# Relative bias rows stored three heads at a time, in blocks two to four of stage one

## The chip, the cores and the metric

One core of a Trainium2 chip runs the whole program in one launch. The metric is the device time of that core in microseconds. Three runs of the kernel before gave 3175.7, 3193.27 and 3194.81 us, median 3193.27. The engines are PE (TensorE, matmuls; PEld is its weight load), DVE (VectorE), ACT (ScalarE), POOL (GpSimd) and SP (SyncE), which issues nearly all DMAs here, in one queue and in program order.

## The reference

One layer of a hybrid encoder over 2048 prompt tokens and 8 x 16 sample tokens, width 1024, everything in float32. What the change touches is the bias of group B's attention: a learned value per head and clipped relative distance.

```python
def rel_bias_matrix(rel_bias, qpos, kpos):
    d = jnp.clip(qpos[:, None] - kpos[None, :], -(CHUNK - 1), REL_MAX) + (CHUNK - 1)
    return rel_bias.astype(jnp.float32)[:, d]
...
s = jnp.einsum('bqhd,bkhd->bhqk', qc, kc).astype(jnp.float32) * (DH ** -0.5) + bias
```

There are 8 heads, and `rel_bias` has 320 values a head. Around it the layer is: modulation of the norm by a conditioning vector, one projection `h @ w_in` (1024 x 3592), a gated delta rule with a causal convolution on group A, band attention on group B, `w_out`, and a feed-forward of width 4096 with squared ReLU.

## The kernel before, in words

Float32 matmuls are made of three products each: every operand is split into a high and a low part, and `mm3` (L162 to L164) or its written-out copies (L519 to L521, L1482 to L1484) multiply high by high, high by low and low by high.

**Weights** come in pieces of 512 KB (`weights`, from L165). SP loads the float32 piece into a ring of three tiles `raw` (L174), ACT casts the high part into a ring of four tiles `w` (L175), and POOL subtracts to get the low part (L82). In the first block SP also stores the low parts of `w_in` in DRAM (L184, `s_w_in`); later blocks load these back (L179) and POOL does not subtract again.

**Stage one** (`phase1`) opens with the modulation vectors out of `w_mod` (pieces `raw0`, loaded at L282), then goes through 17 token tiles of 128 in six blocks: [0, 1, sample], [2, 3, 4], [5, 6, 7], [8, 9, 10], [11, 12, 13], [14, 15]; `bi` is the index of the block. For a block, `proj_a` makes group A's projections: first the gates of one half (`psg`, whose results go to DRAM as `s_sg` at L500), then 12 column pieces (`psq`, 24 matmuls of 128x384 each), each followed on DVE and ACT by the convolution (L79, tile `y`) and on PE by transposes (`ptq`, L554). `proj_b` makes group B's. Blocks three and five hold back their `proj_b`. The gated delta rule of a block (`gdn`) runs as a background lane among the next block's matmuls. The token tiles of the next block are loaded (L373, tile `x`), normed (statistics `bst` on DVE at L378, the root on POOL, the scaling on ACT), transposed (L346, `psh`) into tiles `htmp`, a ring of two, and split into the one tile `hT`, which all matmuls of the block read. PSUM has a ring of three tiles for the results of matmuls.

**Stage two** (`phase2`) does attention, `w_out` and the feed-forward for five blocks of tiles. It reads the bias rows: `bias<-s_bias` from 896.8 us on, `bias_s<-s_bs` at 2464.0 us.

**The bias table.** `rel_bias` (from L1092, called at L1062 once, at block two) loads all eight heads' rows (L1097), lays them out reversed and extended to 768 values a head in a tile of the ring `big` (a memset at L1098, copies on DVE at L1099 and L1100), writes this to DRAM (`s_ext`, L1101), and from there two DMAs from DRAM to DRAM spread it: `s_bias` (L1102, for each head 128 rows of 640 values, each row starting one value earlier) and `s_bs` (L1103, for each head 16 rows of 528).

**Order.** The kernel is written as one program; a scheduler then sets the order on every engine by its own estimate of times, and starts work early where its tile's ring is free. The ring `big` is not used before the first solve, so the scheduler moved the table of block two to the very start of the program, among the modulation's loads.

Of the kernel before, what the change touches and what calls it, by code (L numbers as in the profile page):

```python
# [8 lines left out]
F32 = mybir.dt.float32  # L9
# [5 lines left out]
P = 128  # L15
D = 1024
# [5 lines left out]
SL = 16  # L22
AH = 4
BH = 8
# [4 lines left out]
REL = 320  # L29
EXT = 768  # L30
# [11 lines left out]
def bcast(ap, axis, n):  # L42
    dims = [list(x) for x in ap.ap]
    dims.insert(axis, [0, n])
    return bass.AP(tensor=ap.tensor, offset=ap.offset, ap=dims)


def dram_ap(ap, offset, dims):
    return bass.AP(tensor=ap.tensor, offset=ap.offset + offset, ap=[list(d) for d in dims])


class Trunk:
# [975 lines left out]
    def phase1(self):  # L1028
        nc, tc = self.nc, self.tc
        with ExitStack() as st:  # L1030
            P_ = lambda name, **kw: st.enter_context(tc.tile_pool(name=name, bufs=1, **kw))
            right = ExitStack()
            R_ = lambda name, bufs=1, **kw: right.enter_context(tc.tile_pool(name=name, bufs=bufs, side="right", **kw))
            self.p1, self.hp, self.qp = (P_(x) for x in ("p1c", "p1h", "p1q"))
            self.bp = R_("p1b")
            self.ps = R_("p1ps", 3, space=bass.MemoryType.PSUM)
            pst = ExitStack()
            self.pa = pst.enter_context(tc.tile_pool(name="p1pa", bufs=5 - GP, side="right", space=bass.MemoryType.PSUM))
            self.patag = "pa"
            self.nt = max(len(b) for b in BLOCKS1)  # L1040
            self.nx, self.nA, self.inplace = 3, 4, True
            self.hT = self.p1.tile([P, KT, 2, self.nt * P], F32R, name="hT1")
            with tc.tile_pool(name="p0", bufs=1, side="right") as p0:
                xs = self.modulation_start([(sec, q, u) for q in range(4) for sec in (1, 0) for u in range(2)],
                                           BLOCKS1[0], p0)
            self.mod_todo = [(sec, q, u) for sec in (2, 3, 4, 5) for q in range(4) for u in range(2)]
            self.tp = R_("p1t")
            self.cp = pst.enter_context(tc.tile_pool(name="p1a", bufs=1, side="right"))
            self.phase1_consts()
            S0 = self.tp.tile([P, AH, P], F32, tag="S", name="S", bufs=1)  # L1050
            nc.vector.memset(S0, 0.0)
            self.S = S0
            B = BLOCKS1
            ca = lambda b: 24 * (512 + 1536) * len(B[b])
            cb = lambda b: 24 * 1536 * len(B[b])
            last = len(B) - 1
            self.load_hT(B[0], xs, 0, 1)
            for bi, tiles in enumerate(B):
                self.bi = bi
                self.keep["w_in"] = bi == 0  # L1060
                if bi == 1:
                    self.rel_bias()  # L1062
                self.drain_to(bi - 2)
                self.mix = bi == last
                blk = self.proj_a(tiles, self.hT, B[bi + 1] if bi in LATE else ())
                if bi == last:
                    break
                self.gdn(blk, tiles, bi)
                self.pace(0.95 * (cb(bi) * (bi not in LATE) + ca(bi + 1)), 6000)
                if bi not in LATE:  # L1070
                    self.proj_b(tiles, self.hT, B[bi + 1])
            pst.close()
            self.pa = R_("p1pa2", 1, space=bass.MemoryType.PSUM)
            self.ap2 = R_("p1att", 1, space=bass.MemoryType.PSUM)
            self.ap = R_("p1at")
            self.queue(self.attention_first(BLOCKS2[0]), 1 + BH + BH // 2 * len(BLOCKS2[0]) + BH + 2, lane=2)
            self.queue(self.conv_gen(), 6, lane=1)
            self.gdn(blk, tiles, last)
            rest = [last] + list(LATE)
            self.pace(0.85 * sum(cb(b) for b in rest))  # L1080
            for b, nb in zip(rest, rest[1:] + [None]):
                self.mix = b == last
                self.proj_b(B[b], self.hT, B[nb] if nb is not None else ())
            self.drain()
            nc.sync.dma_start(self.o["gdn_prompt"][0, 0].rearrange("h k v -> k h v"), self.S)
            right.close()
        self.pa, self.patag = self.gp, "g"
        self.ap = self.ctx.enter_context(tc.tile_pool(name="p2a", bufs=1, side="right"))
        self.ap2 = self.ctx.enter_context(tc.tile_pool(name="p2att", bufs=1, space=bass.MemoryType.PSUM, side="right"))


    def rel_bias(self):  # L1092

        nc = self.nc
        x = self.hp.tile([P, D], F32, tag="big", name="ext", bufs=2)
        ext, rev = x[0:BH, 0:REL], x[32:32 + BH, 0:EXT]
        nc.sync.dma_start(ext, self.i["rel_bias"][0])  # L1097
        nc.vector.memset(rev[:, EXT - 64:], 0.0)  # L1098
        nc.vector.tensor_copy(rev[:, EXT - 64 - REL:EXT - 64], ext[:, ::-1])  # L1099
        nc.vector.tensor_copy(rev[:, 0:EXT - 64 - REL], bcast(ext[:, REL - 1], 1, EXT - 64 - REL))  # L1100
        nc.sync.dma_start(self.s_ext, rev)  # L1101
        nc.sync.dma_start(self.s_bias, dram_ap(self.s_ext, P, [[EXT, BH], [-1, P], [1, 640]]))  # L1102
        nc.sync.dma_start(self.s_bs, dram_ap(self.s_ext, P, [[EXT, BH], [-1, SL], [1, 528]]))  # L1103

    def softmax(self, ap, ps, bias, n):

# [494 lines left out]
```

## Time and profile before

| | us |
|---|---|
| median of three runs | 3193.27 (3175.7 to 3194.81) |
| the profiled execution, its own time | 3181.62 |
| its span, first to last instruction | 3179.9 |
| PE busy in the span | 3046.9 (96%) |
| DVE / ACT / POOL busy | 1764.0 / 1472.8 / 644.5 |

The profile is one execution taken by the hardware profiler. Busy time of an engine excludes waits. A wait is put down to what released it. "DMA share" is the mean busy share of the 16 DMA engines, and PEclk the granted TensorE clock as a part of full speed. The mean granted clock of this execution is 0.985.

### The profile page before, as it was taken

The page shows a single profiled execution, that of the slowest core. Times are in us where ns is not written, and L with a number is a line of the kernel's source. Part 1 is how long each engine was busy: PE and PEld are TensorE (multiplying, and loading weights), DVE is VectorE, ACT ScalarE, POOL GpSimd, SP SyncE. Part 2 cuts the span into 40 slices and gives each one's busy share as a digit, 9 for nine tenths or more (in the row PEclk, how much of TensorE's full clock was granted, in tenths as well). Part 3 has the DMA queues.
Part 4 walks back from the last instruction along what each step waited for, and adds up shares of the span by engine and source line. Part 5 has one row for each costly group of instructions (what it writes and reads, how often), then busy time and mean ns, then how long its engine had stood idle before and what let it go on. Part 6 is the DMA issues. An engine that isn't in the chain of part 4 may idle for free.

```text
span 3179.9 us, 52984 instructions
## 1 busy us (share of the span) xinstructions
PE 3046.9 (96%) x19649; PEld 2701.7 (85%) x19649; DVE 1764.0 (55%) x4222; ACT 1472.8 (46%) x2803; POOL 644.5 (20%) x517
## 2 busy tenths in 40 slices
PE   6999999999889989999999999999999999999998
PEld 4998989899889878888999888888988877888887
DVE  4775677667878663674356752454745433442223
ACT  3654545555466555545455353444354333333222
POOL 3631211121342247653222200000000000000000
PEclk9999999999999989999999999999999999999999
DMA  8798897888788778876777765666666676856654
GB/s 289 239 294 268 258 284 228 253 250 248 234 268 264 214 229 277 254 250 231 253 238 244 238 214 181 197 193 204 232 198 200 214 236 219 273 173 194 193 190 139
DMA packets 625947, 735.88 MB, mean 231 GB/s; under 512 B 59328, under 2 KB 483248, under 8 KB 623640
## 3 DMA queue, kind: packets, MB, share of 16 engines
q1 hardware_dynamic: 619928, 701.03, 70.1%
q0 software_dynamic: 5760, 31.46, 3.0%
q8 instruction: 155, 2.54, 0.3%
q14 instruction: 104, 0.85, 0.1%
HBM read 619.74 MB, written 115.52 MB: 231 GB/s over the span
## 4 chain that ended last, share of the span: by engine, by line
PE 70%; DMA 13%; DVE 9%; issue 3%; ACT 3%; POOL 1%; SPq 1%; POOLq 0%; ACTq 0%; DVEq 0%
PE psu L1483 7%; PE psu L1482 7%; PE psu L1484 7%; PE psd L164 7%; PE psd L162 7%; PE psd L163 7%; PE psb L163 2%; DMA raw<-in_w_up_dram 2%; PE psb L162 2%; PE psb L164 2%; PE pv L1286 2%; PE psS L1268 2%; PE psq L519 1%; PE psq L521 1%; PE psq L520 1%
## 5 line engine op out<-in xcount | busy, mean ns | idle before, releaser
L175 ACT CAST w<-raw 128x1024 fp32r<-128x1024 f32 (+1 forms) x528 | 552.1, 1047 | 387.1 <-PE psd L164 214.1
L1482 PE MATMUL psu<-hT,w 128*128 128x512 f32 (+2 forms) x1328 | 470.1, 356 | 1.9 <-ACT hT L104 1.7
L1484 PE MATMUL psu<-hT,w 128*128 128x512 f32 (+2 forms) x1328 | 468.5, 354 | 1.4 <-DMA w<-s_w_up 1.4
L1483 PE MATMUL psu<-hT,w 128*128 128x512 f32 (+2 forms) x1328 | 469.2, 354 | 0.4 <-DVE hT L82 0.3
L82 POOL TENSOR_TENSOR w<-raw,w 128x1024 fp32r<-128x1024 f32 (+1 forms) x162 | 391.6, 2427 | 351.3 <-ACT w L175 285.3
L162 PE MATMUL psd<-w,u 128*128 128x512 f32 x1088 | 430.9, 396 | 0.4 <-DVE y L82 0.3
L164 PE MATMUL psd<-w,u 128*128 128x512 f32 x1088 | 429.8, 396 | 0.0
L163 PE MATMUL psd<-w,u 128*128 128x512 f32 x1088 | 426.8, 392 | 2.1 <-POOL w L82 2.1
L79 DVE SCALAR_TENSOR_TENSOR psu<-psu,r 128x512 f32<-128x512 f32 (+2 forms) x160 | 98.9, 618 | 447.0 <-ACT r L92 446.9
L82 DVE TENSOR_TENSOR y<-y,psd 128x512 f32<-128x512 f32 x238 | 162.4, 685 | 260.3 <-PE psd L164 259.3
L1484 PEld LDWEIGHTS psu<-hT,w 128*128 128x128 f32 x1328 | 250.5, 189 | 33.2 <-DMA w<-s_w_up 1.7
L1482 PEld LDWEIGHTS psu<-hT,w 128*128 128x128 f32 x1328 | 250.1, 189 | 33.0 <-ACT hT L104 2.5
L1483 PEld LDWEIGHTS psu<-hT,w 128*128 128x128 f32 x1328 | 250.7, 189 | 31.9 <-issue 1.3
L92 ACT ACTIVATE r<-psu 128x512 f32<-128x512 f32 (+2 forms) x160 | 85.4, 534 | 375.7 <-issue 214.0
L163 PEld LDWEIGHTS psd<-w,u 128*128 128x128 f32 x1088 | 204.6, 188 | 47.8 <-POOL w L82 2.8
L164 PEld LDWEIGHTS psd<-w,u 128*128 128x128 f32 x1088 | 204.2, 188 | 46.4 <-issue 0.4
L162 PEld LDWEIGHTS psd<-w,u 128*128 128x128 f32 x1088 | 204.4, 188 | 43.8 <-DVE y L82 1.0
L162 PE MATMUL psb<-w,hT 128*128 128x256 f32 x816 | 236.0, 290 | 0.9 <-ACT hT L104 0.8
L163 PE MATMUL psb<-w,hT 128*128 128x256 f32 x816 | 234.7, 288 | 0.9 <-DMA w<-s_w_in 0.9
L164 PE MATMUL psb<-w,hT 128*128 128x256 f32 x816 | 233.4, 286 | 1.9 <-DVE hT L82 1.8
L519 PE MATMUL psq<-hT,w 128*128 128x384 f32 (+1 forms) x576 | 196.9, 342 | 8.1 <-ACT ba L499 8.1
L521 PE MATMUL psq<-hT,w 128*128 128x384 f32 (+1 forms) x576 | 193.6, 336 | 0.2 <-DMA w<-s_w_in 0.2
(315 smaller groups left out, 6459.5 us busy)
## 6 DMA issues: line engine op xcount, KB each, us to landing
raw<-in_w_up_dram SPq DMA_DIRECT2D x160, 512.0 KB
raw<-in_w_down_dram SPq DMA_DIRECT2D x160, 512.0 KB
raw<-in_w_in_dram SPq DMA_DIRECT2D x156, 512.0 KB
w<-s_w_down SPq DMA_DIRECT2D x128, 512.0 KB
w<-s_w_in SPq DMA_DIRECT2D x117, 512.0 KB
w<-s_w_up SPq DMA_DIRECT2D x96, 512.0 KB
raw<-in_w_out_dram SPq DMA_DIRECT2D x40, 512.0 KB
x<-in_x_prompt_dram SPq DMA_DIRECT2D x38, 512.0 KB
```

The costliest lines, as they stand in the source:

```text
L79: (eng or self.nc.vector).scalar_tensor_tensor(out, in0, scalar, in1, op0, op1)
L82: (eng or self.nc.vector).tensor_tensor(out, in0, in1, op)
L92: self.nc.scalar.activation(out, in_, func, **kw)
L162: mm(out, lh, rh, start=first, stop=False)
L163: mm(out, lh, rl, start=False, stop=False)
L164: mm(out, ll, rh, start=False, stop=last)
L175: nc.scalar.copy(w[:, 0, 0:n], r)
L519: mm(pc, wh, hT[:, k, 0, 0:T], start=(k == 0), stop=False)
L521: mm(pc, wl, hT[:, k, 0, 0:T], start=False, stop=(k == KT - 1))
L1482: mm(ps[:, c0:c1], wh, h2[:, k, 0, c0:c1], start=(k == 0), stop=False)
L1483: mm(ps[:, c0:c1], wh, h2[:, k, 1, c0:c1], start=False, stop=False)
L1484: mm(ps[:, c0:c1], wl, h2[:, k, 0, c0:c1], start=False, stop=(k == KT - 1))
```

## The change

The table is made in three calls, at the starts of blocks two, three and four, for heads 0 to 2, 3 to 5 and 6 to 7. The tile is now one of the ring `htmp` (512 values a partition in place of 1024), so a head's 768 values lie in two partitions: 512 in `lo` and 256 in `hi`. Each call has one load, three copies and a memset on DVE, two writes to `s_ext`, and one DMA each into `s_bias` and `s_bs`. Bytes written to `s_bias` and `s_bs` are the same in sum.

```diff
-                if bi == 1:
-                    self.rel_bias()
+                if 1 <= bi <= 3:
+                    self.rel_bias(3 * bi - 3, min(3 * bi, BH))
...
-    def rel_bias(self):
+    def rel_bias(self, h0, h1):
...
-        x = self.hp.tile([P, D], F32, tag="big", name="ext", bufs=2)
-        ext, rev = x[0:BH, 0:REL], x[32:32 + BH, 0:EXT]
-        nc.sync.dma_start(ext, self.i["rel_bias"][0])
-        nc.vector.memset(rev[:, EXT - 64:], 0.0)
-        nc.vector.tensor_copy(rev[:, EXT - 64 - REL:EXT - 64], ext[:, ::-1])
-        nc.vector.tensor_copy(rev[:, 0:EXT - 64 - REL], bcast(ext[:, REL - 1], 1, EXT - 64 - REL))
-        nc.sync.dma_start(self.s_ext, rev)
-        nc.sync.dma_start(self.s_bias, dram_ap(self.s_ext, P, [[EXT, BH], [-1, P], [1, 640]]))
-        nc.sync.dma_start(self.s_bs, dram_ap(self.s_ext, P, [[EXT, BH], [-1, SL], [1, 528]]))
+        m, k = h1 - h0, EXT - 64 - REL
+        x = self.hp.tile([P, 4, P], F32, tag="htmp", name="ext", bufs=2).rearrange("p a b -> p (a b)")
+        ext, lo, hi = x[0:m, 0:REL], x[32:32 + m], x[64:64 + m, 0:EXT - 512]
+        rev = ext[:, ::-1]
+        nc.sync.dma_start(ext, self.i["rel_bias"][0][h0:h1])
+        nc.vector.tensor_copy(lo[:, 0:k], bcast(ext[:, REL - 1], 1, k))
+        nc.vector.tensor_copy(lo[:, k:], rev[:, 0:512 - k])
+        nc.vector.tensor_copy(hi[:, 0:EXT - 576], rev[:, 512 - k:])
+        nc.vector.memset(hi[:, EXT - 576:], 0.0)
+        nc.sync.dma_start(self.s_ext[h0:h1, 0:512], lo)
+        nc.sync.dma_start(self.s_ext[h0:h1, 512:], hi)
+        o = h0 * EXT + P
+        nc.sync.dma_start(self.s_bias[h0:h1], dram_ap(self.s_ext, o, [[EXT, m], [-1, P], [1, 640]]))
+        nc.sync.dma_start(self.s_bs[h0:h1], dram_ap(self.s_ext, o, [[EXT, m], [-1, SL], [1, 528]]))
```

In the changed kernel the lines of `rel_bias` are L1099 (load), L1100 to L1102 (copies), L1103 (memset), L1104 and L1105 (`s_ext`), L1107 (`s_bias`) and L1108 (`s_bs`).

What the scheduler made of it. On SP's queue near the start of the program, between the last loads for the modulation and the first weights, the difference is (minus: before only):

```order
 L174 DMA raw<-in_w_in_dram 128x4x264 x2
 L174 DMA raw<-in_w_in_dram 128x8x128
-L1097 DMA ext<-in_rel_bias_dram 8x320
 L282 DMA raw_207<-in_w_mod_dram 128x4x256
 L373 DMA x<-in_x_prompt_dram 128x1024
 L184 DMA s_w_in<-w 128x1056
 L174 DMA raw<-in_w_in_dram 128x8x128
-L1101 DMA s_ext<-ext 8x768
 L184 DMA s_w_in<-w 128x1056
 L174 DMA raw<-in_w_in_dram 128x8x128
```

The load of the rows and the write of the table are gone from here; some rows later so are the two DMAs that spread it (L1102 and L1103), which stood ahead of the third load of `x`.

On SP's queue of the changed kernel, in block two, at the first call (heads 0 to 2; `A<-s_U` are the solved 32x32 blocks of block one coming back, `s_sg` a gate of block two):

```order
L1104 DMA s_ext<-ext 3x512
L1105 DMA s_ext<-ext 3x256
L500 DMA s_sg<-sgw 128x256
L174 DMA raw<-in_w_in_dram 128x8x128
L179 DMA w<-s_w_in 128x1024
L174 DMA raw<-in_w_in_dram 128x8x128
L179 DMA w<-s_w_in 128x1024
L174 DMA raw<-in_w_in_dram 128x8x128
L1107 DMA s_bias<-s_ext 384x1x640
L1108 DMA s_bs<-s_ext 48x1x528
L666 DMA A<-s_U 32x4x32 x12
L560 DMA s_kt<-kvw 128x128 x3
```

In the kernel before, the same place has the gate, the weights and `A<-s_U` and nothing else. The second and third calls stand in the same way at the gates (`s_sg`) of blocks three and four.

On DVE of the changed kernel, at the same call (`ta` and `Ds` are the solve of block one, `sgw` the last gate of block two, `y` the first convolution of block two):

```order
L82 TENSOR_TENSOR ta<-Z,Ds 128x16
L82 TENSOR_TENSOR Ds<-Ds,ta 128x16
L79 SCALAR_TENSOR_TENSOR sgw<-th,psg 128x256
L1100 COPY ext<-ext 3x384
L1101 COPY ext<-ext 3x128
L1102 COPY ext<-ext 3x192
L79 SCALAR_TENSOR_TENSOR y<-psq,cw,y 128x384
```

Before, the convolution followed the gate at once. The rest of the order differs in many places from the second column piece of block one until the second block of stage two, since the scheduler set it anew; the kinds and numbers of matmuls are the same.

## Rows read from the trace of the kernel before

**Rows 1.** The page's part 1, busy time by engine.
```profile
PE 3046.9 (96%) x19649; PEld 2701.7 (85%) x19649; DVE 1764.0 (55%) x4222; ACT 1472.8 (46%) x2803; POOL 644.5 (20%) x517
```

**Rows 2.** Chain of waits, 28 to 100 us: start, us, what.
```profile
33.54 7.19 DMA ext<-in_rel_bias_dram
...
40.76 2.60 DVE ext L1099
43.36 2.41 DVE ext L1100
...
46.84 1.11 PE psh L346 x4
...
62.39 13.29 DMA x<-in_x_prompt_dram
...
78.10 0.34 DVE sgw L79
```

**Rows 3.** Timeline of all engines, 36 to 48 us.
```profile
38.38 7.19 POOL L82 TENSOR_TENSOR w<-raw,w 128x1056 fp32r<-128x1056 f32 x3 [8.95 <-ACT w L175]
...
42.08 1.08 PE L288 MATMUL mps<-raw,cT 128*32 128x256 f32 x8 [2.90 <-DMA raw<-in_w_mod_dram]
```

**Rows 4.** Timeline of SP's queue, 0 to 90 us: start, time to issue.
```profile
33.54 2.21 SPq L1097 DMA_DIRECT2D ext<-in_rel_bias_dram  x1
...
50.38 0.84 SPq L1102 DMA_DIRECT2D s_bias<-s_ext  x1
51.28 8.49 SPq L1103 DMA_DIRECT2D s_bs<-s_ext  x1
...
62.39 5.70 SPq L373 DMA_DIRECT2D x<-in_x_prompt_dram  x1
```

**Rows 5.** DMA issues by line, 0 to 100 us.
```profile
s_bias<-s_ext SPq DMA_DIRECT2D x1, 2560.0 KB
...
s_bs<-s_ext SPq DMA_DIRECT2D x1, 264.0 KB
```

**Rows 6.** Timeline of PE, 64 to 100 us.
```profile
70.25 0.33 PE L521 MATMUL psq<-hT,w 128*128 128x384 f32 x1
78.68 0.69 PE L519 MATMUL psq<-hT,w 128*128 128x384 f32 x1 [8.10 <-ACT ba L499]
...
82.61 0.34 PE L519 MATMUL psq<-hT,w 128*128 128x384 f32 x1
...
84.54 0.34 PE L521 MATMUL psq<-hT,w 128*128 128x384 f32 x1
```

**Rows 7.** Stretches: busy us by engine, granted clock, DMA share, GB/s.
```profile
57.00:62.00 5.00, 3.53 (x21) 3.06 (x22) 3.50 (x10) 2.92 (x7) 0.56 (x1) 1.00 0.52 207
...
70.00:79.00 9.00, 0.90 (x5) 0.58 (x4) 3.29 (x7) 2.63 (x9) 2.35 (x1) 0.81 1.00 342
...
100.00:150.00 50.00, 50.00 (x342) 49.36 (x341) 36.11 (x87) 30.53 (x89) 31.30 (x15) 1.00 0.73 227
...
215.00:235.00 20.00, 20.00 (x125) 19.34 (x124) 13.80 (x50) 10.66 (x26) 2.04 (x2) 1.00 1.09 324
...
385.00:410.00 25.00, 25.00 (x155) 22.98 (x154) 16.79 (x54) 8.17 (x18) 3.86 (x3) 1.00 1.01 303
...
485.00:515.00 30.00, 29.95 (x271) 28.74 (x270) 21.01 (x63) 17.54 (x44) 2.06 (x2) 1.00 0.75 219
```

**Rows 8.** Chain of waits, 0 to 250 us: loads of weights in block two.
```profile
207.62 6.85 DMA w<-s_w_in
...
230.02 5.98 DMA raw<-in_w_in_dram
...
242.74 8.42 DMA raw<-in_w_in_dram
```

**Rows 9.** What PE waited for, whole span: us, times, longest.
```profile
PE psb L163 <- DMA w<-s_w_in: 0.9, 1, 0.9
...
PE psq L521 <- DMA w<-s_w_in: 0.2, 1, 0.2
```

## The prediction

> **What bounds the kernel now.** I read the page's busy times first, then the chain of waits at the start (where the table is made), then the timelines of PE, DVE and SP around it, then the stretches into which the three new calls fall. PE is busy 3046.9 of 3179.9 us [rows 1], so only the 133.0 us in which it stands can be won, and anything new that stops it is paid in full. From 100 to 150 us PE is busy all the time [rows 7]; the start is not like that. There the chain of waits runs through the bias table itself: it waits for the load of the rows (7.19 us), stands through the two copies on DVE (2.60 and 2.41 us), and later waits 13.29 us for a load of `x` that was issued behind the table's spreading [rows 2]. PE stands for 8.10 us at 78.68 [rows 6]. In the stretches of the new calls PE loses nothing: 20.00 of 20, 25.00 of 25 and 29.95 of 30 us, but the DMA engines are full in two of them, 1.09 and 1.01, and 0.75 in the third [rows 7].
>
> **What goes from the start.** Three terms.
>
> First, the copies. DVE is in order, and behind the two copies stands the norm's scaling of `htmp`, on which PE's transposes at 46.84 wait [rows 2]. Without the copies PE is ready for these when its previous matmuls end, 42.08 + 1.08 = 43.16 [rows 3]. That is 46.84 - 43.16 = 3.7 us. POOL's subtractions in the same stretch [rows 3] go on as before and aren't waited for there.
>
> Second, the load of `x`. SP spends 0.84 us on the issue of `s_bias` and 8.49 us on that of `s_bs`, and the load of `x` is issued only at 62.39 [rows 4], behind 2560 + 264 KB of the table [rows 5]. DVE stands at its statistics until it lands at 62.39 + 13.29 = 75.68; the third gate behind it is done at 78.44, and only that frees a PSUM tile for PE at 78.68 [rows 2, 6]. Without the table the load is issued some 9 us earlier and has 2.8 MB less ahead of it; at 342 GB/s [rows 7] these alone are 8.5 us. So the 8.10 us go. Something new is late next: in the new order the small gate arithmetic of block one, which PE now needs after its third column piece, stands on DVE behind the same statistics, ahead of the results that free PSUM. I take 2 us for that, so this term is 6.1; its bounds are 0 (the gate arithmetic takes it all) and 8.1.
>
> Third, the slow matmuls after the stop. From 78.68 to 82.61 PE makes 12 matmuls in 3.93 us, and from 82.61 to 84.54 eleven in 1.93, or 0.175 each [rows 6]. The granted clock of 70 to 79 us is 0.81 [rows 7], a mean of the two levels (2.4 and 1.2 GHz) after an idle stretch. Twelve at 0.175 are 2.1, so 1.8 us go with the stop.
>
> Sum at the start: 3.7 + 6.1 + 1.8 = 11.6 us, bounds 3.7 and 13.6.
>
> **What comes back, on the queue.** The same bytes are now moved in blocks two to four: 3/8, 3/8 and 2/8 of them, each time as `s_bias` and then `s_bs` on SP's queue ahead of loads of weights and of the solved blocks. The only price in the trace is the load of `x` behind the whole table: 13.29 us [rows 2], where loads of the same size in block two take 5.98 to 8.42 us [rows 8], about 7. So the whole table delays what stands behind it by 13.3 - 7 = 6.3 us. If the price goes with the heads, the three calls delay by 2.4, 2.4 and 1.6, together 6.3. If a call costs the same whatever its heads (descriptors, the stop of SP's queue), it is 18.9. The low end is 0: PE has waited 0.9 and 0.2 us for stored low parts of `w_in` in the whole span [rows 9], so loads arrive ahead of need, and a delay can vanish in that lead. Nearest in kind is the one write that the trace shows, in a full queue; two of three places are as full. I take 6.3.
>
> **What comes back, on DVE.** Each call's copies wait on DVE for the load of their rows, and DVE is in order: behind them stand the gate or the first convolution, which free PSUM for PE. The load of rows takes 7.19 us from issue to landing [rows 2], and in all three calls it is issued at a gate of the block, with the copies due a gate or two later. PE has PSUM for three results, and a column piece is 24 matmuls at 0.175, or 4.2 us [rows 6]; so most of a wait is covered. I take 1 us a call, 3 in all; bounds 0 and 3 x 7.2 = 21.6. The copies themselves: nine, each of at most 384 values, against two of 320 and 384 at 2.60 and 2.41 us [rows 2]. By these rows nine cost 9 x 2.5 = 22.5 us of DVE, with DVE busy 13.80 of 20, 16.79 of 25 and 21.01 of 30 us there [rows 7]: it has the room for 7.5 us a call spread over some gates, and I cost them at nothing, hidden beside PE's matmuls. Each of the two copies before is as long as one of POOL's three subtractions (7.19 us for three, 2.40 each [rows 3]) and ends within 0.2 us of the end of one. The Trainium skill (SBUF — State Buffer, Who interferes with whom) says that VectorE copies in a two-port mode and GpSimd hold a shared port pair exclusively, for a whole instruction; this trace agrees. By that rule the new copies are long only where POOL works; POOL is busy 2.04 of 20, 3.86 of 25 and 2.06 of 30 us there [rows 7], so the sum by it is 9 x 2.4 x 0.11 = 2.4 us of DVE, an estimate, in place of 22.5. Either way the forecast stays. The ring `htmp` is not waited for: its next users after a call come with the next block's tiles, some ten column pieces or a whole `proj_b` later.
>
> **Sum.** -11.6 + 6.3 + 3.0 = -2.3 us against the profiled execution's own 3181.62: 3179.3. That execution lies 11.65 us under the median of the three runs, and these spread over 19.1 us. A median of the changed kernel may fall anywhere in that spread, so I add half of the 11.65, 5.8, to this and to every case below: 3185.
>
> **Rivals.** (a) The write of a few heads holds the queue as long as that of eight. In 57 to 62 us, with the table's DMAs just issued and SP still busy on one of them, the DMA share is 0.52 at 207 GB/s [rows 7]: about half of the engines work, while loads wait for their issue. If a head's rows go by one engine, three heads take as long on three engines as eight on eight, and every load by 128 partitions needs these three too. Price: 13.3 us a call; less one column piece of cover, 4.2, at the two full places is 9.1 each, and half, 4.5, at the third: 22.7. Time: 3181.6 - 11.6 + 22.7 + 3.0 + 5.8 = 3201.5. Uncovered it is 39.9, or 3218.7. It decides once weights land later than their lead. Against it: later blocks' weights have some lead [rows 9], and no row shows which engines a transfer used. The Trainium skill (DMA: Bandwidth & Descriptors, Why a DMA increments its semaphore by 16 and not by 1) states that a transfer is split over the largest number of engines up to 16 that divides the slowest dimension of both its sides. By it the table went over eight engines before and goes over three, three and two now, each with one head's rows. The share of 0.52 would fit.
>
> (b) DVE stands at the copies for the whole 7.2 us, three times, and PE with it: 21.6 in place of 3.0 gives 3203.8. For it: the queue is full where the rows are loaded. Against: PSUM for three results.
>
> (c) The start gains only the copies' 3.7, because the gate arithmetic or a weight is late next: 3181.6 - 3.7 + 6.3 + 3.0 + 5.8 = 3193.0. For it: the DMA share is 1.00 in 70 to 79 us [rows 7].
>
> (d) Nothing comes back, because the lead of the weights hides it: 3181.6 - 11.6 + 5.8 = 3175.8. For it: rows 9. Against: the shares of 1.09 and 1.01.
>
> The new order of everything after the first block adds or takes a few us in each case; no row prices it.
>
> **Chances.** Forecast 0.30, (a) 0.25, (b) 0.10, (c) 0.15, (d) 0.20. The range for 8 in 10 reaches from (d) with the order's spread below it, 3165, to (a) and (b) with a part of the uncovered case, 3210. The forecast's own range is 3175 to 3195. A measurement of this kernel tells about 1%, 31.9 us of the median, from no change. No case lies below 3161.3, and only (a) uncovered comes near 3225.2; I give 0.05 to faster and 0.06 to slower, for what the new order may do besides, and 0.89 to no difference.
>
> **What would show it.** Right: the chain at the start no longer names `ext`; PE's stop of 8.10 us is 2 or less; PE reaches the state of 100 us about 11 us earlier; in blocks two to four DVE waits for `ext` some us three times, and PE's new stops after the `s_bias` writes sum to about 6. Case (a) would show loads of weights landing 13 us after issue behind each write, with PE waiting for them; (b) PE standing for DVE at each call; (c) a stop of similar length near 70 us with another name; (d) no new waits of PE after 200 us. The forecast is wrong if the start gains less than 4 us or the three calls cost more than 15.

## The result and the profile after

The changed kernel takes 3231.49 us (median of 4 runs, 3230.36 to 3235.47) against 3190.07 us before (4 runs, 3175.7 to 3194.81): a ratio of 1.014, 95% interval 1.0105 to 1.0175, so it is slower by some 41 us. The forecast of 3185 was wrong, and the time lies outside the range (3165 to 3210). The profiled execution has a span of 3233.8 us, 53.9 more than that of before.

The page's busy times come first; beside [rows 1]:

```profile
PE 3072.0 (95%) x19649; PEld 2724.3 (84%) x19649; DVE 1765.9 (55%) x4231; ACT 1474.1 (46%) x2803; POOL 644.5 (20%) x517
```

PE makes the same 19649 matmuls, but is busy 25.1 us longer (3072.0 - 3046.9), and it stands for 161.8 us in place of 133.0, 28.8 more. Against this profile of before the loss is thus half stops and half matmuls that take longer. Not all of the second half belongs to the calls: with matmuls paired as in the next table, 17.4 of the 25.1 us lie between 750 and 1400 us, where no table is written, and a second profile of before (from an experiment below) has 8.5 of them too.

To see where it falls, I paired each operation of ACT with its like in before (same tiles, same count) and took the difference of their starts; the table has medians over stretches of 35 operations, at the time in before's profile. The second profile of before shows how far two executions of one kernel differ.

| at (us, before) | 150 | 211 | 274 | 371 | 435 | 553 | 733 | 932 | 1341 | 3056 |
|---|---|---|---|---|---|---|---|---|---|---|
| after | -4.2 | -3.5 | +2.9 | +2.7 | +11.4 | +36.0 | +36.4 | +41.7 | +58.4 | +53.6 |
| after, second profile | -1.6 | -0.9 | +5.0 | +7.7 | +15.6 | +35.7 | +39.9 | +43.5 | +58.5 | +57.2 |
| before, second profile | -2.6 | -2.7 | -2.7 | -2.1 | -2.9 | -2.0 | -3.8 | -5.7 | +6.6 | +2.4 |

The start gains a few us only; three steps between 211 and 553 us take about 40; some 20 more are lost between 733 and 1341, of which before's own second execution lost 10 too.

The three steps are the three calls. The stretches that answer to [rows 7], with those right behind the calls (same columns):

```profile
215.00:235.00 20.00, 20.00 (x122) 19.31 (x121) 14.88 (x49) 10.94 (x27) 2.04 (x2) 1.00 1.08 319
235.00:262.00 27.00, 17.41 (x108) 15.03 (x107) 6.75 (x14) 6.16 (x15) 0.00 (x0) 0.81 0.41 129
385.00:410.00 25.00, 24.78 (x157) 22.28 (x155) 18.56 (x53) 11.30 (x25) 6.42 (x4) 1.00 0.71 217
410.00:435.00 25.00, 14.14 (x66) 12.24 (x67) 10.85 (x35) 7.05 (x17) 1.04 (x1) 0.73 0.89 272
```

PE still loses next to nothing while a call's rows are copied (20.00 of 20, 24.78 of 25 us); in the 27 us behind the first call it is busy 17.41, and the DMA share falls from 1.08 to 0.41. The DMA view of 225 to 262 us says what happens to it. Its two rows are 40 slices of 0.93 us: the busy share of 16 engines in tenths, and GB/s.

```profile
DMA  9998999999521111212322211211300348989999
GB/s 247 229 307 226 356 328 339 370 354 309 148 80 75 77 80 77 95 75 93 106 90 93 81 75 76 68 20 23 50 14 2 89 142 111 266 322 356 360 408 353
```

For about 14 us the engines move mostly 75 to 95 GB/s, with a share of 0.1 to 0.2: about three of 16. The third call's, of two heads, in 515 to 560 us:

```profile
DMA  2920002104411111679921499999999993100005
GB/s 42 347 92 2 0 0 91 31 0 64 190 50 52 48 50 52 166 193 378 353 98 50 112 295 290 313 340 372 334 299 358 359 334 109 43 17 0 0 0 195
```

Now it is 48 to 52 GB/s: two engines. In [rows 7] the eight heads went at 207 GB/s with a share of 0.52. Each time it is 25 to 26 GB/s a head (207/8, 76/3, 50/2).

SP's queue at the first two calls, which answers to [rows 4]:

```profile
228.91 2.00 SPq L1107 DMA_DIRECT2D s_bias<-s_ext  x1
230.96 7.01 SPq L1108 DMA_DIRECT2D s_bs<-s_ext  x1
238.02 15.20 SPq L666 DMA_DIRECT2D A<-s_U  x12
...
401.14 0.74 SPq L1107 DMA_DIRECT2D s_bias<-s_ext  x1
401.95 6.22 SPq L1108 DMA_DIRECT2D s_bs<-s_ext  x1
408.27 1.40 SPq L179 DMA_DIRECT2D w<-s_w_in  x1
409.73 1.02 SPq L174 DMA_DIRECT2D raw<-in_w_in_dram  x1
410.81 6.12 SPq L179 DMA_DIRECT2D w<-s_w_in  x1
```

Before took 8.49 us to issue `s_bs` of eight heads; three heads' takes 7.01 and 6.22. Then the queue stands again over whatever is issued next: 15.20 us over the twelve small loads of solved blocks, which before went out in 8.22:

```profile
231.54 8.22 SPq L666 DMA_DIRECT2D A<-s_U  x12
```

What PE waited for behind the three calls (us, times, longest; 225 to 300, 400 to 470 and 515 to 610 us):

```profile
PE ptT L789 <- DMA A<-s_U: 8.7, 2, 8.4
...
PE psq L521 <- DMA w<-s_w_in: 10.5, 1, 10.5
...
PE ptO L876 <- DVE z L79: 10.0, 1, 10.0
```

Three stops, one a call, each for something loaded behind the write: solved blocks, low parts of weights, and in the third (here DVE's `z` by name, but the chain of waits leads over DVE and POOL to a load `X<-s_vt` of 8.20 us) stored rows. Last, the clock between the second and the third call:

```profile
493.21 1.11 PE L346 MATMUL psh<-ident,x 128*128 128x128 f32 x4 [3.39 <-DVE modT L324]
...
490.00:521.00 31.00, 26.57 (x213) 23.43 (x214) 16.07 (x47) 14.00 (x30) 1.12 (x2) 0.51 0.59 184
```

PE stopped for 3.39 us at 493.21, behind a run of short matmuls, and for 31 us the granted clock is 0.51, near the lower of its two levels (1.2 of 2.4 GHz). It is busy 26.57 us there; by the clock alone up to 13 would be lost without standing (26.57 x 0.49, an estimate), and by the same 213 matmuls in before, which take 16.5 us, it is about 10. The slow stretch differs from execution to execution: in the second profile of the changed kernel the clock is 0.50 from 500 to 510 us and 0.77 from 510 to 520. A stop of 3.4 to 4.4 us at this work is in all four profiles in which writes of two or three heads go by few engines in blocks two to four; of the kernels below whose writes use 8 or 16 engines, only the one with its call in block three has one, of 2.0.

### The profile page after: what moved, and what is told of

The parts are those of the page before. It is cut to its first block, busy times and chain, and to the rows that moved or that the text cites. A ratio compares the mean times of both kernels' runs of the same rounds, so it can differ in the third digit from the quotient of the medians.

```text
span 3233.8 us, 53013 instructions
## 1 busy us (share of the span) xinstructions
PE 3072.0 (95%) x19649; PEld 2724.3 (84%) x19649; DVE 1765.9 (55%) x4231; ACT 1474.1 (46%) x2803; POOL 644.5 (20%) x517
## 4 chain that ended last, share of the span: by engine, by line
PE 71%; DMA 12%; DVE 9%; ACT 3%; issue 2%; POOL 2%; SPq 1%; POOLq 0%; ACTq 0%; DVEq 0%
PE psu L1487 7%; PE psu L1488 7%; PE psu L1489 7%; PE psd L164 7%; PE psd L162 7%; PE psd L163 7%; PE psq L519 2%; DMA raw<-in_w_up_dram 2%; PE psq L520 2%; PE psq L521 2%; PE pv L1291 2%; PE psS L1273 2%; PE pso L162 2%; PE pso L163 2%; PE pso L164 2%
## 5 line engine op out<-in xcount | busy, mean ns | idle before, releaser
L521 PE MATMUL psq<-hT,w 128*128 128x384 f32 (+1 forms) x576 | 194.3, 337 | 10.5 <-DMA w<-s_w_in 10.5
```

The costliest lines, as they stand in the source:

```text
L521: mm(pc, wl, hT[:, k, 0, 0:T], start=False, stop=(k == KT - 1))
```

## The experiments

Theory E: a write goes over as many DMA engines as it has heads, always the same first ones, takes 13 us whatever its heads, and what is loaded behind it over all 16 waits for those. Rivals: the place in the queue or SP's stop, whatever the engines (Q, P); the scheduler's new order (O). All times are medians beside runs of before on the same chip.

| run | us | ratio to before, 95% |
|---|---|---|
| one_call | 3199.92 | 1.0035 (1.0015 to 1.0055) |
| start_three_writes | 3222.17 | 1.0095 (1.0065 to 1.0125) |
| three_calls_16 | 3209.65 | 1.0069 (1.0049 to 1.0088) |
| one_call_16 | 3197.80 | 1.0032 (1.0013 to 1.0051) |
| before_again | 3188.92 | 1.0012 (0.9991 to 1.0034) |
| after_again | 3236.53 | 1.0149 (1.0113 to 1.0185) |
| start_16 | 3194.36 | 1.0019 (0.9999 to 1.0040) |
| one_call_16_block3 | 3208.46 | 1.0061 (1.0044 to 1.0079) |
| block1_call_8 | 3181.67 | 0.9990 (0.9976 to 1.0005) |
| block1_call_16 | 3180.48 | 0.9989 (0.9974 to 1.0003) |
| three_calls_pool_queue | 3225.69 | 1.0135 (1.0107 to 1.0163) |
| three_calls_sub_on_dve | 3223.80 | 1.0117 (1.0079 to 1.0155) |

### The split alone, at the old place: start_three_writes

```diff
-        nc.sync.dma_start(self.s_bias, dram_ap(self.s_ext, P, [[EXT, BH], [-1, P], [1, 640]]))
-        nc.sync.dma_start(self.s_bs, dram_ap(self.s_ext, P, [[EXT, BH], [-1, SL], [1, 528]]))
+        for h0, h1 in ((0, 3), (3, 6), (6, BH)):
+            o = h0 * EXT + P
+            nc.sync.dma_start(self.s_bias[h0:h1], dram_ap(self.s_ext, o, [[EXT, h1 - h0], [-1, P], [1, 640]]))
+            nc.sync.dma_start(self.s_bs[h0:h1], dram_ap(self.s_ext, o, [[EXT, h1 - h0], [-1, SL], [1, 528]]))
```

> The kernel before, with the spreading at its old place at the start, but each of s_bias and s_bs written by three DMAs of three, three and two heads. Theory E: a head is 13 us on its engine; if every write takes the same first engines, the three take 39 us, the load of x lands up to 26 us later and PE's stop of 8.10 us grows to as much as 34, 3205 to 3220; if the writes spread over different engines, they run side by side and it is 3188 to 3197. Rivals Q (the place) and O (the order): the place and the order are those of before, so 3185 to 3197, with 1 or 2 us for four more issues.

Measured 3222.17 us, 36 over before by the medians and 30 by the ratio: just above E's 3205 to 3220, and far from the rivals' 3185 to 3197. The DMA view of 50 to 100 us (slices of 1.25 us):

```profile
DMA  9992111111112111111111111111398711587969
GB/s 394 374 299 104 76 80 76 78 80 76 78 80 86 70 77 80 76 78 78 78 78 78 78 78 76 64 49 53 145 324 222 249 51 53 97 316 272 399 155 341
```

Three writes issued within 25 us run one after the other: 76 to 80 GB/s for 28 us, and about 50 for the last, of two heads. Were they on different engines, they would run side by side, as the eight heads of [rows 7] did at 207. SP's queue shows the load of `x` of [rows 4] pushed from 62.39 to 86.33:

```profile
47.11 1.79 SPq L1104 DMA_DIRECT2D s_bias<-s_ext  x1
48.95 8.52 SPq L1105 DMA_DIRECT2D s_bs<-s_ext  x1
57.52 1.53 SPq L1104 DMA_DIRECT2D s_bias<-s_ext  x1
59.09 12.60 SPq L1105 DMA_DIRECT2D s_bs<-s_ext  x1
71.74 1.53 SPq L1104 DMA_DIRECT2D s_bias<-s_ext  x1
...
86.33 6.37 SPq L373 DMA_DIRECT2D x<-in_x_prompt_dram  x1
```

By paired operations it is 28.2 us behind at 150 us and 25.8 at 733: two further writes of 13 us. So the split of the write costs by itself, with no new place.

### Fewer calls, or more engines: one_call, three_calls_16, one_call_16

In one_call the three calls are one, in block two, with eight heads on eight engines:

```diff
-                if 1 <= bi <= 3:
-                    self.rel_bias(3 * bi - 3, min(3 * bi, BH))
+                if bi == 1:
+                    self.rel_bias(0, BH)
```

> The changed kernel, but with one call of all eight heads in block two in place of three calls. Theory E (a write goes over as many DMA engines as it has heads: eight here, 13 us once, with half of the bandwidth left to the loads behind it): the start keeps its gain of 5.7 us, the one write costs 0 to 10, no load of weights or of solved blocks lands late enough to stop PE for 8 us or more in 225 to 300 us; 3175 to 3200 us. Rival Q (SP's queue is held by the issue of the table wherever it stands in a full block, whatever the engines): one call costs a third of the about 60 us that three cost, 20, so 3198 to 3212. Rival O (the scheduler's new order after the first block costs it, not the writes): 3225 or more, since the order is new here too.

three_calls_16 keeps the three calls and makes the slowest dimension of each write 16, which takes 16 copies of the table in DRAM; the values are the same:

```diff
-        nc.sync.dma_start(self.s_ext[h0:h1, 0:512], lo)
+        nc.sync.dma_start(self.s_ext[:, h0:h1, 0:512].rearrange("a h c -> h a c"), bcast(lo, 1, 16))
...
-        nc.sync.dma_start(self.s_bias[h0:h1], dram_ap(self.s_ext, o, [[EXT, m], [-1, P], [1, 640]]))
+        for h in range(h0, h1):
+            nc.sync.dma_start(self.s_bias[h].rearrange("(a b) c -> a b c", a=16), dram_ap(self.s_ext, h * EXT + P, [[BH * EXT - P // 16, 16], [-1, P // 16], [1, 640]]))
...
```

> The changed kernel with its three calls at their places; the table lies 16 times in DRAM, and each head's s_bias is one DMA whose slowest dimension is 16 groups of eight rows (s_bs: 16 rows), so that all 16 engines take part; the same bytes are read and written, plus 0.37 MB for the copies. Theory E: a call's write takes 2.5 us of all engines in place of 13 of three; PE's stops of 8.7, 10.5 and 10.0 us go or shrink to 3 or less, 3175 to 3200. Rival Q (place and SP's queue): two more issues a call, so 3228 or more. Rival O (order): 3222 to 3235.

one_call_16 is both together.

> One call of all eight heads in block two, over 16 engines (the table 16 times in DRAM, one DMA a head). Theory E: the write takes 6.6 us of all engines, the loads behind it come up to 7 us later, nothing is starved for 13: 3175 to 3195, within 8 us of the single call over eight engines. Rival Q: 3198 or more, and above the single call over eight, for it issues seven DMAs more. Rival O: 3222 or more.

The single call on eight engines comes to 3199.92, at the upper edge of E's 3175 to 3200, where rivals Q (3198 to 3212) and E overlap; its trace decides more than its time. The DMA view of 225 to 262 us of one_call:

```profile
DMA  9968989999999555555655565556022347899999
```

0.5 for 13 us: eight engines, as at the start of before. PE waits 3.9 us for `A<-s_U` there in place of 8.7, and by paired operations the call costs 5.3 us (-1.9 at 211, +3.4 at 274), where Q has 20; from 733 to 1341 us this profile loses 17 more. Rival O (3225 or more) is out.

three_calls_16 comes to 3209.65: 22 us less than the changed kernel with the same calls at the same places, which neither rival allows (3222 or more), but 10 above E's range. Until 733 us it is 8.9 us behind before, where the changed kernel is 36.4. What PE still waits for behind the three calls:

```profile
PE ptq L554 <- DVE vT L79: 2.7, 1, 2.7
...
PE psq L521 <- DMA w<-s_w_in: 6.1, 1, 6.1
...
PE ptq L554 <- DVE kq L79: 1.9, 1, 1.9
```

8.7 and 10.0 are gone; 10.5 is 6.1. The remedy has its own price: the table's copies are written by three partitions, and the DMA share is 0.1 to 0.5 for about 4 us while they go. After 733 us, where no table is written, its profile loses 24.3 us more, most of its 33.2. one_call_16, 3197.80, is within 8 us of one_call, as E says, but 2.8 above E's 3195, and only 0.2 below Q's 3198; its interval overlaps one_call's, so that this time decides nothing between the two. By paired operations its call costs about 5 us, as over eight engines: PE no longer waits for `A<-s_U` there, but 4.8 us for `vT`.

### Two profiles of the same kernel: before_again, after_again

Both are the kernels as they are.

> The kernel before, unchanged, for a second profile of it. In the runs so far PE loses 8 to 20 us more between 780 and 1250 us than in the first profile of before, also in the kernel whose order of work is that of before (three writes at the start). Theory S (that stretch differs from execution to execution): this profile reaches 1250 us 5 us or more later than the first one did, at equal progress up to 780 us. Theory K (it is what the changes do to the later order): within 3 us of the first profile all along. Time by either 3180 to 3195 us.

> The changed kernel, unchanged, for a second profile and more timed runs. Theory E: again three stretches of about 13 us at a DMA share of 0.1 to 0.2 behind the three writes, and PE 35 to 45 us behind before at 600 us; 3222 to 3240 us. If the stops of 8 to 10 us were chance, one or more of them is missing and PE is less than 20 us behind at 600 us.

after_again repeats the result (1.0149) and its three stops: 8.4, 10.0 and 10.1 us. before_again has the time of before, but its profile is 3.8 us ahead at 733 us and 6.6 behind at 1341. So Theory S holds, if not from the equal progress that it set out from: executions differ by 10 us in this stretch, and the first profile of before was a good one there. It does not hold for all of the loss: after loses 22.0 from 733 to 1341, three_calls_16 26.1, start_three_writes 19.8 with the order of before. What else costs 10 to 15 us there is not settled. A new order alone doesn't: the two kernels with the call in block one, below, lose 10.6 and 1.5 there. PE is stopped there by many waits of 1 to 3 us with different names, and the granted clock of 1150 to 1250 us is 0.83 and 0.85 in the two profiles of after, against 0.91 and 0.88 in those of before for nearly the same work, 1100 to 1200 us.

### Where the table may stand: start_16, one_call_16_block3, block1_call_8, block1_call_16

start_16 is before with the table over 16 engines at its place. one_call_16_block3 is one_call_16 with `if bi == 2`. In the last two the single call (over 8 and over 16 engines) is made in block one:

```diff
-                if 1 <= bi <= 3:
-                    self.rel_bias(3 * bi - 3, min(3 * bi, BH))
                 self.drain_to(bi - 2)
                 self.mix = bi == last
                 blk = self.proj_a(tiles, self.hT, B[bi + 1] if bi in LATE else ())
+                if bi == 0:
+                    self.rel_bias(0, BH)
```

> The kernel before with its table at the start, but over 16 DMA engines (the table 16 times in DRAM, one DMA a head). Theory E: the 2.8 MB take 6.6 us of all engines in place of 13.1 of eight; the load of x behind them lands 3 to 6 us earlier after its issue, PE's stop of 8.10 us shrinks to 3 to 6; 3180 to 3190 us. Rival: it is the bytes that hold up the load, at whatever share of the engines, or the seven more issues of 0.55 us each that take back what the engines give; the stop stays at 7 to 12, 3186 to 3196 us.

> One call of all eight heads over 16 engines, in block three in place of block two. Theory E: over 16 engines a call costs 0 to 8 us wherever it stands; 3185 to 3203 us, within 8 us of the same call in block two (3197.8). Rival P (it is block two's full queue that costs, and the order behind it): the solved blocks of block two aren't delayed now, and it comes out at 3180 to 3190 us.

> The changed kernel's code with one call of all eight heads, made when block one's columns have been issued; its writes stand in SP's queue right behind the third load of x, over eight engines, where PE is busy and the DMA share is about 0.7 (100 to 150 us). Theory E (a write costs what the loads behind it lack in lead): no load of x or of solved blocks is behind it, so the start keeps its gain of 2 to 5 us and the call costs 0 to 3; 3180 to 3190 us, ratio 0.997 to 1.001. Rival P (any table work inside the blocks costs 10 or more, as one call in block two did): 3196 to 3206 us.

> The same call in block one, over 16 engines (the table 16 times in DRAM, one DMA a head). Theory E: with room in the queue the engines no longer matter; within 5 us of the same call over eight engines, 3180 to 3192 us. Rival P: 3196 to 3206 us.

start_16 missed E's 3180 to 3190 by 4 us and lies inside its rival's 3186 to 3196: PE's stop of 8.10 does shrink to 3.53, as E said, but a new one of 6.41 comes ahead of it, for the second load of `x`. That load stands behind the write of the 16 copies into `s_ext`: SP takes 3.59 us for the load of weights after that write and 3.99 for that of `x`, where before it took 0.38 and 0.33. So the remedy seems to delay what stands behind it, and nothing is won. one_call_16_block3 missed as well, by 5: until 371 us it is 4.9 ahead, at 435 it is 0.5 behind, at 492 10.5, and it loses 27 more from 733 to 1341. In the first 5 us a stop of 2.2 us for a low part behind the write is new, and one of 3.5 for `kq` has its like in before (2.9); the rest is the clock, 0.74 from 400 to 420 us against 0.91 in before. The next 10 are a stop of 2.0 and a granted clock of 0.51 from 480 to 500 us. So 16 engines alone don't make a call free, and E as I put it was too kind.

The call in block one costs nothing that the time shows. SP's queue of block1_call_8 has the last load of `x` ahead of the table:

```profile
52.67 1.32 SPq L373 DMA_DIRECT2D x<-in_x_prompt_dram  x1
...
64.97 0.88 SPq L1107 DMA_DIRECT2D s_bias<-s_ext  x1
65.90 6.93 SPq L1108 DMA_DIRECT2D s_bs<-s_ext  x1
```

DVE waits 0.5 us for `x` in place of 6.5, and no load that PE is seen to wait for stands behind the write. PE still stands for 7.4 us, for `kq` behind the gate arithmetic on DVE, where before has 8.10 and the changed kernel 4.76. Its waits from 50 to 100 us, and the first of the call's copies, which stands on DVE ahead of that arithmetic:

```profile
PE ptq L554 <- DVE kq L79: 8.0, 2, 7.4
...
60.92 2.14 DVE L1100 COPY ext<-ext 8x384 f32<-8x384 f32 x1
```

3181.67 and 3180.48 us: about 50 us less than the changed kernel, and 0.1% under before, which these runs don't tell from none (both intervals reach 1). Eight engines or 16 make no difference there.

### Another queue: three_calls_pool_queue

```diff
-        nc.sync.dma_start(self.s_bias[h0:h1], dram_ap(self.s_ext, o, [[EXT, m], [-1, P], [1, 640]]))
-        nc.sync.dma_start(self.s_bs[h0:h1], dram_ap(self.s_ext, o, [[EXT, m], [-1, SL], [1, 528]]))
+        nc.gpsimd.dma_start(self.s_bias[h0:h1], dram_ap(self.s_ext, o, [[EXT, m], [-1, P], [1, 640]]))
+        nc.gpsimd.dma_start(self.s_bs[h0:h1], dram_ap(self.s_ext, o, [[EXT, m], [-1, SL], [1, 528]]))
```

> The changed kernel, three calls of three, three and two heads, but s_bias and s_bs are issued on POOL's DMA queue in place of SP's. The same few engines hold the same 13 us of packets, but SP is not stopped while it issues, and on each engine the packets of the two queues can take turns. Theory E1 (it is the engines: any load over 16 waits for the three busy ones): the stops of 8 to 10 us stay at 5 or more, 3215 to 3240 us. Theory E2 (it is the order within one queue: loads stand behind the table's packets): loads on SP's queue take turns with the table's, their delay is halved or less, the stops shrink to 4 or less, 3190 to 3212 us.

3225.69 us: E1. SP no longer issues the table, and is held all the same, over the loads of solved blocks:

```profile
231.08 19.42 SPq L666 DMA_DIRECT2D A<-s_U  x12
```

PE's first stop is again 8.4 us and the third 9.0. The second, for a low part of weights, is gone; PE waits 5.0 us for `kq` there, as it does for 2.9 in before. So for two stops of three it is neither SP's own issue of the table nor the order within one queue, but the engines; for the second that stays open.

### What ate the gain at the start: three_calls_sub_on_dve

In the changed kernel the 8.10 us stop is gone, but PE stands for 4.76 us at 77.30, for the gates. Timelines of PE, DVE and POOL, 60 to 80 us:

```profile
77.30 0.49 PE L616 MATMUL psd<-g,incl 128*128 128x4 f32 x2 [4.76 <-DVE g L82]
...
65.27 1.43 DVE L82 TENSOR_TENSOR x<-ba,dtb 128x12 f32<-128x12 f32 x1 [1.62 <-ACT ba L499]
66.73 2.33 DVE L79 SCALAR_TENSOR_TENSOR u<-x 128x12 f32<-128x12 f32 x1
69.09 0.17 DVE L87 TENSOR_SCALAR x<-x 128x12 f32<-128x12 f32 x1
...
70.69 2.22 DVE L82 TENSOR_TENSOR z<-u,z 128x12 f32<-128x12 f32 x1
...
64.26 4.77 POOL L82 TENSOR_TENSOR w<-raw,w 128x1024 fp32r<-128x1024 f32 x2 [1.09 <-ACT w L175]
70.47 2.40 POOL L82 TENSOR_TENSOR w<-raw,w 128x1024 fp32r<-128x1024 f32 x1 [1.44 <-ACT w L175]
```

Twelve values a partition take 0.17 us, or 1.43 to 2.33 where POOL subtracts; 66.73 + 2.33 = 69.06 is within 0.04 us of the end of POOL's pair (64.26 + 4.77 = 69.03), 70.69 + 2.22 = 72.91 of that of the next (70.47 + 2.40 = 72.87).

```diff
+        self.nsub = getattr(self, "nsub", 0) + 1
-        self.tt(w[:, 1, 0:n], r, w[:, 0, 0:n].bitcast(F32), ALU.subtract, eng=nc.gpsimd)
+        self.tt(w[:, 1, 0:n], r, w[:, 0, 0:n].bitcast(F32), ALU.subtract, eng=nc.vector if 6 <= self.nsub <= 8 else nc.gpsimd)
```

> The changed kernel, with three subtractions for low parts of w_in in block one (the sixth to the eighth, which POOL made from 64 to 73 us) on DVE in place of POOL. It asks why the start gained so little: in the changed kernel three operations of the gate arithmetic on 128x12 values take 1.43, 2.33 and 2.22 us on DVE where their like take 0.17, each ends with one of POOL's subtractions, and PE then waits 4.76 us for the gates' result. Theory H (DVE is held while POOL subtracts): the three take 0.2 each, the wait of 4.76 shrinks to 2.5 or less although DVE now has three subtractions of about 1 to 1.4 us more; PE is 2 to 5 us earlier at 100 us. Theory A (the arithmetic is as long as that by itself, or waits for its inputs): the three stay above 1 us and the wait at 4 or more. The three writes cost what they did, so the whole is 3222 to 3237 us by either.

Theory H: with the subtractions on DVE (1.23 us each, where POOL's take 2.4), the three operations are back at 0.17, and the wait of 4.76 is gone:

```profile
66.93 0.17 DVE L82 TENSOR_TENSOR x<-ba,dtb 128x12 f32<-128x12 f32 x1
67.13 0.17 DVE L79 SCALAR_TENSOR_TENSOR u<-x 128x12 f32<-128x12 f32 x1
...
70.59 0.16 DVE L82 TENSOR_TENSOR z<-u,z 128x12 f32<-128x12 f32 x1
```

PE has a new wait of 4.2 us for `kq` a little later, however, and stands 5.2 us ahead of before at 150 us, where the two profiles of the changed kernel were 4.2 and 1.6 ahead. So about 1 to 3.6 us of the 4.76 come through. The whole time, 3223.80, isn't told from after's: the ratios' intervals overlap.

## Why the prediction was wrong, step by step

**The failed step is the price on the queue.** I took 6.3 us for all three calls ("if the price goes with the heads"), with 18.9 as the upper bound. By paired operations the three calls cost 40.2 us in the first profile of after (36.0 at 553 us, from -4.2 at 150) and 37.3 in the second. Both of the prediction's own signs of being wrong came: three calls above 15, a start below 4 us. The price doesn't go with the heads: each call holds its engines for 13 us, and with that the mechanism of rival (a) is shown, by the rates of 75 to 80 and 48 to 52 GB/s, by start_three_writes (which splits and doesn't move) and by three_calls_16 (which moves and doesn't concentrate). I gave (a) 0.25 and a cover of a column piece. That its uncovered 39.9 is near what came is in part luck: the stops behind the three writes are 8.7, 10.5 and 10.0 us, near its covered 9.1, and the rest is mostly the clock, which (a) doesn't have. The Trainium skill's rule (DMA: Bandwidth & Descriptors, Why a DMA increments its semaphore by 16 and not by 1) gave the engines right: 8, 3, 3 and 2. I treated the rule as a rival because no row showed the engines of a transfer, though a share of 0.52 at 207 GB/s stood there.

**Why the lead covered so little.** I read the small waits of [rows 9] as lead in the whole span. The lead that counts is that of the loads issued in those 13 us, and the ones that PE reaches first (solved blocks, low parts, stored rows) had 3 to 5 us of it (13.3 less the three stops). The nearest price, 13.29 us for `x` behind the table, was measured with half of the engines free; behind three busy ones a load over all 16 waits just as long, and SP can't issue what follows either.

**The clock.** The prediction priced slow matmuls at the start (1.8 us) and none behind new stops. By paired matmuls PE is busy 10.9 us longer than in before from 225 to 610 us, 7.5 in the second profile: 20 to 27% of what the calls cost. In the first profile about 10 of it lie in the row of 490 to 521 us.

**The start.** The copies' wait of 3.7 us is gone, but the second profile of before has 1.4 there, so more than half of it was chance: the first copy started about 0.3 us before the end of one of POOL's subtractions there and took 0.47 us in place of 2.60. The stop of 8.10 is gone as predicted; I allowed 2 us for the gate arithmetic that is late next, and it took 4.76, held by POOL's subtractions. The 1.8 us of slow matmuls didn't go either: behind the shorter stop the granted clock is 0.54 (77 to 82 us), as it was 0.55 behind the old one (78 to 83 us). So the first half of the forecast failed as well: at 150 us the two profiles of after stand 4.2 and 1.6 ahead of the first of before (mean 2.9), but the second of before stands 2.6 ahead of it too (mean of both 1.3), so the gain is near 1.6, not 11.6. That is less than rival (c) took.

**DVE.** Rival (b) is out, and the 3 us for waits were too much: DVE waited 0.6 us for `ext`, once in the three calls. Nine copies cost 0.2 to 0.35 us each, not 2.5:

```profile
L1100 DVE COPY ext<-ext x3: 349/350/350, 218.9 to 521.7; 3x384 f32<-3x384 f32 x2, 2x384 f32<-2x384 f32 x1
```

So the two copies before, at 2.60 and 2.41, were held by POOL, as the Trainium skill has it (SBUF — State Buffer, Who interferes with whom), and that section's rule for an instruction with two inputs in SBUF, which I didn't use, covers the gate arithmetic: it contends with a GpSimd instruction that reads SBUF, and the trace agrees (1.43 to 2.33 us in place of 0.17).

**What was right.** The chain at the start no longer names `ext`, the 8.10 us stop went, PE is ahead until the first call, and the test that I wrote for case (a), loads landing 13 us after issue with PE waiting, comes close at two calls: PE goes on 11.6 us after the first `A<-s_U` is issued (238.02 to 249.63), and 9.4 to 12.0 after a `w<-s_w_in` (two are issued, at 408.27 and 410.81; PE goes on at 420.24). At the third, the load that PE's stop goes back to was itself issued late, at 544.53.

## What to carry to other kernels

Before a DRAM transfer is split by its outer dimension, look at its rate in the trace: if it moves at a fraction of the full rate, that fraction may be its outer dimension's share of the engines, and a third of the work then takes as long on a third of the engines, while every transfer over all of them waits. Give such a transfer an outer dimension that uses all engines, or put it where nothing that is needed soon stands behind it; here the second was worth more and cost nothing that the time shows. And price a new stop of TensorE with the slower clock that can come behind it: around the three calls the same matmuls were busy 7.5 to 10.9 us longer, beside some 30 us of standing.

## What was not expected of the hardware

- Writes of three heads, issued one behind the other, went on the same three engines at 76 to 80 GB/s for 28 us, with the other engines nearly idle: for writes from SP's queue, engines aren't taken in turn. Another issuing queue didn't help: SP then took 19.42 us over twelve small loads that take 8.22 in before.
- One head of `s_bias` is 128 rows of 2560 bytes, 0.33 MB; at 25.6 GB/s that is 12.8 us, and neither two, three nor eight heads changed that rate.
- A DVE operation on 12 values a partition took up to 2.33 us, in place of 0.17, beside a subtraction on POOL, and DVE makes that subtraction itself in 1.23 us against POOL's 2.4.
- The two profiles of before stay within 3.8 us of each other up to 733 us, and then drift apart, from -3.8 to +6.6 at 1341 us: one profile doesn't price a change of 10 us there.
